# The delta rule stage of a two-block model: decayed query-key products on VectorE, decayed keys on ScalarE

## The chip, the cores and the metric

The kernel runs on one core of a Trainium2 chip. A core has TensorE (matmuls), VectorE, ScalarE and GpSimd, each with an instruction queue of its own, and SyncE, which issues the transfers here. The metric is the device time of one execution in microseconds (us), shown as the median of repeated runs. Beside the runs one execution was taken down by the hardware profiler; all rows below come from it.

## What is computed

The reference runs a sequence of 512 tokens with 1024 features through two blocks of layers in float32. The change lies in the gated delta rule of the second block, with 16 value heads, 8 query-key heads of 128 features and a chunk length of 64 in the reference. Cut to the rule, it reads:

```python
def gated_delta_rule(q, k, v, g, beta):
    """S_t = exp(g_t) (I - beta_t k_t k_t^T) S_{t-1} + beta_t k_t v_t^T,  o_t = S_t^T q_t."""
...
    g = jnp.cumsum(g, axis=-1)
    decay = jnp.exp(jnp.where(lower, g[..., :, None] - g[..., None, :], -jnp.inf))
    L = jnp.where(strict, jnp.einsum('bhncd,bhnsd->bhncs', kb, k) * decay, 0.0)
    T = lax.linalg.triangular_solve(eye + L, eye, left_side=True, lower=True, unit_diagonal=True)
    u = T @ vb
    w = T @ (kb * jnp.exp(g)[..., None])
    attn = jnp.einsum('bhncd,bhnsd->bhncs', q, k) * decay
    q_dec = q * jnp.exp(g)[..., None]
    k_dec = k * jnp.exp(g[..., -1:] - g)[..., None]
    def step(state, inp):
        v_new = u_n - jnp.einsum('bhcd,bhde->bhce', w_n, state)
        o = q_n @ state + a_n @ v_new
        state = state * gl_n + jnp.einsum('bhcd,bhce->bhde', k_n, v_new)
```

Here `attn` is the decayed query-key product, `q_dec` the decayed queries and `k_dec` the decayed keys. The kernel names them At, qd and kdec, and the decayed key product L is its Am. It uses chunks of 128.

## The kernel before

Activations are kept feature-major, as tiles of 128 features by 512 tokens. Each float32 matmul is made of three products of rounded halves (L145 to L147: high by high, low by high, high by low). A weight tile arrives by DMA, ScalarE casts it to its high half wh (L139) and VectorE subtracts to get the low half wl (L140). Below, a projection row is one such matmul of 128x512 of L145 to L147, and 24 of them make one output tile of a 1024-feature projection in a bank of PSUM.

The delta rule stage is `gdn`, from about 1875 to 2420 us of the span. It goes in eight groups `gi`, each of one query-key head and the two value heads that share it. The functions called for a group are:

- `stage_a`: the projections of q and k, the convolution (L1020 on ScalarE, three L1022 on VectorE, then the tanh L1015 on ScalarE and L1016 on VectorE, which make silu), the norms of q and k, the masked key-key and query-key products (L1100 on TensorE, L1101 on VectorE, into tiles gt), the decay e on ScalarE (L1117, L1119, into a tmp), then for each of two heads Am (L1121, L1122 on VectorE) and At (L1123), the exponentials for qd (L1124), qd (L1127 on GpSimd, one product per head), and the inversion of the unit triangular matrix. The last begins with 15 pairs of small VectorE steps (L1144 product, L1146 sum), has DMAs to shuffle blocks (L1133 to L1156), and ends with small matmuls on TensorE (L1169 to L1207).
- `stage_v`: the projections, the convolution and the silu of the two value heads into cv, transposed on TensorE (L1221) and copied by ScalarE (L1222).
- `stage_b`: the recurrence over four chunks of 128 tokens. A chunk makes kdec (L1240, not for the last chunk), then on TensorE L1248 (state times keys), R on VectorE (L1251), L1254, vnew on ScalarE (L1257), L1261 (kdec times vnew, the new state's sum), L1264 and L1265 (outputs from qd and At), the new state on VectorE (L1271, L1274) and the output oT on ScalarE (L1276). kdec has one buffer, so that the kdec of a chunk waits until L1261 of the chunk before has read the old one.
- `stage_z`, `stage_g` and `stage_o`: the gate, the output norm and the output projection. `norms` transposes (L1036) on TensorE, sums squares on ScalarE (L1038), makes the inverse root on VectorE (L1041 to L1051), and brings it back either by broadcast matmuls (L1057; the first two groups of `stage_a` and the last group's outputs) or by a transpose L1062, a copy L1064 and two DMAs. `stage_g` multiplies the outputs by the gate (L1287, L1288). In `stage_o` the output projection of a group fills a bank, and L1305 on VectorE adds it into h and frees the bank.

Program order is `stage_a(0)`, `stage_a(1)`, `stage_v(0)`, and then for each group `stage_v(gi+1)`, `stage_a(gi+2)`, `stage_b(gi)`, `stage_z(gi)`, `stage_g(gi)`, `stage_o(gi-1)`. A scheduler lays out each engine's queue when the program is built, from this order and its own priorities, and some steps carry a raised priority (`high_priority`: the norms' chain, R, St and L1305). Each engine then runs its queue strictly in order. PSUM banks come from four pools: three for projections ("acc"), two of "sa", two of "sb", one of "mg". The `tmp` tiles rotate through four buffers.

Of the kernel before, what the change touches and what calls it, by code (L numbers as in the profile page):

```python
# [12 lines left out]
AF = mybir.ActivationFunctionType  # L13
# [6 lines left out]
D, S, DFF, KT, P = 1024, 512, 2816, 8, 128  # L20
# [420 lines left out]
def c4(ap, c):  # L441
    return ap[:, c * P:(c + 1) * P]
# [524 lines left out]
def gdn(self, feed0, gate, tail):  # L967
    nc, tc, A = self.nc, self.tc, self.A
    with tc.tile_pool(name="gd", bufs=1) as gd, tc.tile_pool(name="gdd", bufs=1, space=bass.MemoryType.DRAM) as dr:
        def T(name, shape=(P, S), dtype=F32, bufs=None):  # L970
            return gd.tile(list(shape), dtype, name=name, bufs=bufs)
# [103 lines left out]
        def stage_a(gi):  # L1075
# [14 lines left out]
            knat = T("knat", (P, 4, P), bufs=2)  # L1090
# [5 lines left out]
            kkm, qkm = T("gt", bufs=2), T("gt", bufs=2)  # L1096
# [12 lines left out]
            ekd = T("ekd", (P, 2, 4), bufs=2)  # L1109
# [3 lines left out]
            Am, At = T("Am", (P, 8, P), bufs=2), T("At", (P, 8, P), bufs=2)  # L1113
            for a in range(2):
                e = self.tmp()
                for c in range(4):
                    nc.scalar.activation(c4(e, c), gbc[:, a, c * P:(c + 1) * P], AF.Relu, scale=-1.0,  # L1117
                                         bias=gcol[:, c, hs[a]:hs[a] + 1])
                nc.scalar.activation(e, e, AF.Exp, scale=-1.0)  # L1119
                m = Am[:, a * 4:(a + 1) * 4, :]  # L1120
                nc.vector.tensor_mul(m.rearrange("p c i -> p (c i)"), kkm, e)  # L1121
                nc.vector.tensor_mul(m, m, bcol[:, :, hs[a]:hs[a] + 1].to_broadcast([P, 4, P]))  # L1122
                nc.gpsimd.tensor_mul(At[:, a * 4:(a + 1) * 4, :].rearrange("p c i -> p (c i)"), qkm, e)  # L1123
            nc.scalar.activation(gbc, gbc, AF.Exp, bias=ln_qs)  # L1124
            qd = T("qd", (P, 2, S), bufs=2)
            for a in range(2):
# [106 lines left out]
        def stage_b(gi, d, vn):  # L1233
            hs, U, k = d["hs"], d["U"], d["k"]
            oT = T("oT", (P, 2, S))
            St = None
            for c in range(4):
                if c < 3:
                    kdec = T("kdec", (P, 2, P))
                    nc.gpsimd.tensor_mul(kdec, d["knat"][:, c:c + 1, :].to_broadcast([P, 2, P]),  # L1240
                                         d["ekd"][:, :, c:c + 1].to_broadcast([P, 2, P]))
                pp = self.bank("sb")
                if c == 0:
                    R = vn[:, 0]
                else:
                    R = T("R", (P, 2, P))
                    for a in range(2):
                        nc.tensor.matmul(c4(pp, a), c4(k, c), St[:, a, :], start=True, stop=True)  # L1248
                    with tc.high_priority():
                        for a in range(2):  # L1250
                            nc.vector.scalar_tensor_tensor(R[:, a, :], c4(pp, a), neg[:, c, hs[a]:hs[a] + 1],  # L1251
                                                           vn[:, c, a, :], op0=ALU.mult, op1=ALU.add)
                for a in range(2):
                    nc.tensor.matmul(c4(pp, 2 + a), U[:, a * 4 + c, :], R[:, a, :], start=True, stop=True)  # L1254
                w = T("vnew", (P, 2, P), bufs=2)
                for a in range(2):
                    nc.scalar.activation(w[:, a, :], c4(pp, 2 + a), AF.Copy, scale=bcol[:, c, hs[a]:hs[a] + 1])  # L1257
                po = self.bank("sb")
                if c < 3:
                    for a in range(2):  # L1260
                        nc.tensor.matmul(c4(po, 2 + a), kdec[:, a, :], w[:, a, :], start=True, stop=True)  # L1261
                for a in range(2):
                    if c:
                        nc.tensor.matmul(c4(po, a), St[:, a, :], d["qd"][:, a, c * P:(c + 1) * P], start=True, stop=False)  # L1264
                    nc.tensor.matmul(c4(po, a), w[:, a, :], d["At"][:, a * 4 + c, :], start=c == 0, stop=True)  # L1265
                if c < 3:
                    sn = T("St", (P, 2, P), bufs=2)
                    with tc.high_priority():
                        for a in range(2):
                            if c:  # L1270
                                nc.vector.scalar_tensor_tensor(sn[:, a, :], St[:, a, :], d["egl"][:, a, c:c + 1],  # L1271
                                                               c4(po, 2 + a), op0=ALU.mult, op1=ALU.add)
                            else:
                                nc.vector.tensor_copy(sn[:, a, :], c4(po, 2 + a))  # L1274
                    St = sn
                nc.scalar.copy(oT[:, :, c * P:(c + 1) * P], po[:, 0:256].rearrange("p (a d) -> p a d", a=2))  # L1276
            return oT
# [29 lines left out]

        og, last = {}, []
        st = {gi: stage_a(gi) for gi in range(2)}
        vs = {0: stage_v(0)}  # L1310
        for gi in range(8):
            if gi < 7:
                vs[gi + 1] = stage_v(gi + 1)
            if gi < 6:
                st[gi + 2] = stage_a(gi + 2)
            if gi == 0:
                self.late()
            oT = stage_b(gi, st.pop(gi), vs.pop(gi))
            z = stage_z(gi)
            og[gi] = stage_g(gi, oT, z)  # L1320
            if gi:
                stage_o(gi - 1, og.pop(gi - 1))
# [436 lines left out]
```

## Time and profile before

| | us |
|---|---|
| runs, median of 3 | 2773.18 |
| runs, lowest and highest | 2771.43, 2778.86 |
| profiled execution | 2774.42 |
| its span in the trace | 2772.6 |
| mean granted TensorE clock over the span | 0.987 |

The span is the time from the first to the last instruction in the trace; the profiled execution's own time holds 1.8 us more around it. Busy times are given by engine: PE is TensorE, PEld its weight loads, DVE VectorE, ACT ScalarE, POOL GpSimd. An engine's idle time is put down to the event that ended it, its releaser, written with an arrow. PEclk, the granted clock, is given as a share of full speed, 1.00 being the level of 2.4 GHz and 0.50 that of 1.2.

### The profile page before, as it was taken

To read this page: it belongs to the slowest core of one execution; us is meant where nothing else is said; L and a number is where in the kernel's file an instruction comes from. 1 tells how busy PE (TensorE), PEld (TensorE's weight loads), DVE (VectorE), ACT (ScalarE), POOL (GpSimd) and SP (SyncE) were. 2 spreads that over 40 slices of the span, in tenths; PEclk is the share of its full clock that TensorE was granted. 3 is DMA by queue.
4 is the path that set the end of the run, shared out by engine and by line. 5 is a ranking of instruction groups with operands and counts; after the bars stand their busy time and mean duration, and the time that the engine had idled before them with its cause. 6 is when DMAs were issued, how large, how long until landed. Compare 5 with 4: busy or idle time off the path is not lost. (4 is left out here: it accounts for less than half of the span.)

```text
span 2772.6 us, 38299 instructions
## 1 busy us (share of the span) xinstructions
PE 2684.4 (97%) x14903; PEld 2194.3 (79%) x14903; DVE 1723.4 (62%) x3065; ACT 1197.1 (43%) x2200; POOL 237.5 (9%) x224
## 2 busy tenths in 40 slices
PE   8999999999999999999899999998999999999998
PEld 6888878788888888887778888877778788787776
DVE  6454577764545744447965444468777777777776
ACT  4222244532323422224364222255655555577774
POOL 0000002000000000003410000022111111110001
PEclk9999999999999999999999999999999999999999
DMA  5343432243443433223212333223333333132221
GB/s 183 116 144 107 127 97 77 76 144 115 137 119 110 133 112 102 91 91 92 68 39 90 96 94 99 88 75 100 93 107 100 100 114 102 48 101 69 77 66 63
DMA packets 106709, 274.60 MB, mean 99 GB/s; under 512 B 35464, under 2 KB 39552, under 8 KB 106528
## 3 DMA queue, kind: packets, MB, share of 16 engines
q1 hardware_dynamic: 106528, 272.15, 32.5%
q8 instruction: 118, 1.93, 0.3%
q14 instruction: 63, 0.52, 0.1%
HBM read 267.79 MB, written 4.31 MB: 98 GB/s over the span
## 5 line engine op out<-in xcount | busy, mean ns | idle before, releaser
L145 PE MATMUL acc<-xh,wh 128*128 128x512 f32 (+2 forms) x2320 | 913.0, 394 | 18.4 <-ACT xh L186 8.1
L146 PE MATMUL acc<-xl,wh 128*128 128x512 f32 (+1 forms) x2320 | 903.6, 390 | 3.3 <-POOL xl L151 2.4
L147 PE MATMUL acc<-xh,wl 128*128 128x512 f32 (+1 forms) x2320 | 902.4, 389 | 1.7 <-DVE wl L140 1.7
L139 ACT CAST wh<-raw 128x1024 fp32r<-128x1024 f32 (+3 forms) x430 | 438.9, 1022 | 1076.2 <-PE acc L146 714.6
L140 DVE TENSOR_TENSOR wl<-raw,wh 128x1024 fp32r<-128x1024 f32 (+2 forms) x410 | 488.8, 1193 | 71.3 <-ACT wh L139 70.7
L145 PEld LDWEIGHTS acc<-xh,wh 128*128 128x128 f32 (+1 forms) x2320 | 437.8, 189 | 108.4 <-ACT xh L186 8.1
L146 PEld LDWEIGHTS acc<-xl,wh 128*128 128x128 f32 x2320 | 437.7, 189 | 92.7 <-issue 3.7
L147 PEld LDWEIGHTS acc<-xh,wl 128*128 128x128 f32 x2320 | 436.9, 188 | 91.2 <-DVE wl L140 3.2
L146 PE MATMUL acc<-al,wh 128*128 128x512 f32 (+1 forms) x720 | 278.2, 386 | 0.0
L147 PE MATMUL acc<-ah,wl 128*128 128x512 f32 (+1 forms) x720 | 277.7, 386 | 0.0
L145 PE MATMUL acc<-ah,wh 128*128 128x512 f32 (+1 forms) x720 | 277.4, 386 | 0.0
L249 DVE SCALAR_TENSOR_TENSOR h<-acc,h 128x512 f32<-128x512 f32 x128 | 88.4, 690 | 215.3 <-PE acc L147 214.9
L289 DVE TENSOR_TENSOR tmp<-acc,rstd 128x512 f32<-128x512 f32 x88 | 60.8, 691 | 239.2 <-PE acc L147 239.2
L287 DVE TENSOR_TENSOR tmp<-acc,rstd 128x512 f32<-128x512 f32 x88 | 60.8, 691 | 176.3 <-PE acc L147 176.2
L146 PEld LDWEIGHTS acc<-al,wh 128*128 128x128 f32 x720 | 135.2, 188 | 28.8 <-DVE al L151 0.8
L145 PEld LDWEIGHTS acc<-ah,wh 128*128 128x128 f32 x720 | 135.2, 188 | 28.1
L147 PEld LDWEIGHTS acc<-ah,wl 128*128 128x128 f32 x720 | 135.2, 188 | 28.0
L140 POOL TENSOR_TENSOR wl<-raw,wh 128x1024 fp32r<-128x1024 f32 (+1 forms) x20 | 47.8, 2393 | 872.2 <-ACT wh L139 861.4
L145 PE MATMUL acc<-ogh,wh 128*128 128x512 f32 (+1 forms) x256 | 104.4, 409 | 5.4 <-DVE h L1305 3.0
L147 PE MATMUL acc<-ogh,wl 128*128 128x512 f32 (+1 forms) x256 | 99.1, 388 | 0.0
L146 PE MATMUL acc<-ogl,wh 128*128 128x512 f32 (+1 forms) x256 | 99.1, 388 | 0.0
L150 ACT CAST ah<-tmp 128x512 fp32r<-128x512 f32 x88 | 54.9, 624 | 63.8 <-DVE tmp L290 63.8
(450 smaller groups left out, 3462.9 us busy)
## 6 DMA issues: line engine op xcount, KB each, us to landing
raw<-in_wi_dram SPq DMA_DIRECT2D x176, 512.0 KB, 3.6
raw<-in_wo_dram SPq DMA_DIRECT2D x64, 512.0 KB, 3.5
raw<-in_ada_w_dram SPq DMA_DIRECT2D x48, 512.0 KB, 3.6
raw<-in_a_in_dram SPq DMA_DIRECT2D x48, 512.0 KB, 4.1
raw<-in_b_in_dram SPq DMA_DIRECT2D x24, 512.0 KB, 3.6
raw<-in_wo_dram SPq DMA_DIRECT2D x24, 384.0 KB, 3.1
raw<-in_a_out_dram SPq DMA_DIRECT2D x16, 512.0 KB, 3.7
big<-rd SPq DMA_DIRECT2D x13, 512.0 KB, 5.6
```

What stands on the lines that cost most here:

```text
L139: nc.scalar.copy(wh[:, :n], raw[:, :n])
L140: self.lo_eng.tensor_tensor(wl[:, :n], raw[:, :n], f32(wh[:, :n]), op=ALU.subtract)
L145: nc.tensor.matmul(out, ah, bh, start=start, stop=False)
L146: nc.tensor.matmul(out, ah, bl, start=False, stop=False)
L147: nc.tensor.matmul(out, al, bh, start=False, stop=stop)
L150: self.nc.scalar.copy(hi, x)
L249: nc.vector.scalar_tensor_tensor(self.h[m], ps, scale(m), self.h[m], op0=ALU.mult, op1=ALU.add)
L287: nc.vector.tensor_mul(t, pg, rstd)
L289: nc.vector.tensor_mul(u, pu, rstd)
```

## The change

At (L1123) moves from GpSimd to VectorE, with the same operands and shape. kdec, one GpSimd product of 128x256 for both heads (L1240), becomes two ScalarE copies of 128x128, each with a scale per partition taken from ekd (L1241). GpSimd keeps qd, and no other line changes. A group has two At, and three chunks with a kdec: 16 products and 24 kdec (48 copies) in the stage.

```diff
--- before.py
+++ after.py
@@ -1120,7 +1120,7 @@
                 m = Am[:, a * 4:(a + 1) * 4, :]
                 nc.vector.tensor_mul(m.rearrange("p c i -> p (c i)"), kkm, e)
                 nc.vector.tensor_mul(m, m, bcol[:, :, hs[a]:hs[a] + 1].to_broadcast([P, 4, P]))
-                nc.gpsimd.tensor_mul(At[:, a * 4:(a + 1) * 4, :].rearrange("p c i -> p (c i)"), qkm, e)
+                nc.vector.tensor_mul(At[:, a * 4:(a + 1) * 4, :].rearrange("p c i -> p (c i)"), qkm, e)
             nc.scalar.activation(gbc, gbc, AF.Exp, bias=ln_qs)
             qd = T("qd", (P, 2, S), bufs=2)
             for a in range(2):
@@ -1237,8 +1237,8 @@
             for c in range(4):
                 if c < 3:
                     kdec = T("kdec", (P, 2, P))
-                    nc.gpsimd.tensor_mul(kdec, d["knat"][:, c:c + 1, :].to_broadcast([P, 2, P]),
-                                         d["ekd"][:, :, c:c + 1].to_broadcast([P, 2, P]))
+                    for a in range(2):
+                        nc.scalar.activation(kdec[:, a], d["knat"][:, c], AF.Copy, scale=d["ekd"][:, a, c:c + 1])
                 pp = self.bank("sb")
                 if c == 0:
                     R = vn[:, 0]
```

Since each queue is laid out anew, other instructions move too. Three places follow. The first is VectorE's queue in the ramp, while the second group's Am and At are made beside the first group's inversion (L1144, L1146) and ahead of the first value heads' silu (L1016). Before, At is not in it:

```order
L1146 TENSOR_REDUCE ui<-mt 128x2x2
L1122 TENSOR_TENSOR Am<-Am,gbcol 128x512
L1144 TENSOR_TENSOR mt<-ui,big 128x2x3x10
L1016 SCALAR_TENSOR_TENSOR cv<-tmp,cv 128x512
L1146 TENSOR_REDUCE ui<-mt 128x2x3
L1121 TENSOR_TENSOR Am<-gt,tmp 128x512
L1144 TENSOR_TENSOR mt<-ui,big 128x2x3x11
L1122 TENSOR_TENSOR Am<-Am,gbcol 128x512
L1146 TENSOR_REDUCE ui<-mt 128x2x3
L1144 TENSOR_TENSOR mt<-ui,big 128x2x3x12
L1146 TENSOR_REDUCE ui<-mt 128x2x3
L1016 SCALAR_TENSOR_TENSOR cv<-tmp,cv 128x512
```

With the change:

```order
L1144 TENSOR_TENSOR mt<-ui,big 128x2x3x10
L1122 TENSOR_TENSOR Am<-Am,gbcol 128x512
L1146 TENSOR_REDUCE ui<-mt 128x2x3
L1123 TENSOR_TENSOR At<-gt,tmp 128x512
L1144 TENSOR_TENSOR mt<-ui,big 128x2x3x11
L1121 TENSOR_TENSOR Am<-gt,tmp 128x512
L1146 TENSOR_REDUCE ui<-mt 128x2x3
L1122 TENSOR_TENSOR Am<-Am,gbcol 128x512
L1144 TENSOR_TENSOR mt<-ui,big 128x2x3x12
L1123 TENSOR_TENSOR At<-gt,tmp 128x512
L1146 TENSOR_REDUCE ui<-mt 128x2x3
L1016 SCALAR_TENSOR_TENSOR cv<-tmp,cv 128x512
```

Both At now stand in VectorE's queue; two L1121, two L1122, two L1123 and six chain steps come ahead of the first L1016 of cv, where there had been one Am alone. The second L1016 follows after one more chain step, and two L1022 of x come next, ahead of the three of cv; before, the first of cv came two rows after the second L1016.

The second place is TensorE's queue at the output norms of the first group: L1062 transposes the inverse roots (nr), and the last L1036 of the same outputs oT stands some rows ahead of it. Before:

```order
L145 MATMUL acc<-xh_97,wh 128x512
L146 MATMUL acc<-xl_105,wh 128x512
L1062 MATMUL sb<-ident,nr_15115 8x128
L1221 MATMUL sb<-ident,cv 128x128 x4
L147 MATMUL acc<-xh_97,wl 128x512
L1221 MATMUL sb<-ident,cv 128x128 x4
```

With the change:

```order
L145 MATMUL acc<-xh_104,wh 128x512
L1062 MATMUL sb<-ident,nr_15118 8x128
L1221 MATMUL sb<-ident,cv 128x128 x8
L146 MATMUL acc<-xl_112,wh 128x512
L147 MATMUL acc<-xh_104,wl 128x512
L1036 MATMUL sa<-ident,x_15294 128x128 x4
```

Between the last L1036 of oT and this L1062 there are 21 projection rows before and 45 with the change. At the same norms of the next group the count goes from 62 to 22, and there L1169 to L1189 of an inversion and the products L1100 now stand among the rows.

The third place is VectorE's queue around the first four L1305, which add the first group's output projection into h. Before:

```order
L1121 TENSOR_TENSOR Am<-gt,tmp 128x512
L1287 TENSOR_TENSOR oT<-oT,zg 128x512
L1122 TENSOR_TENSOR Am<-Am,gbcol 128x512
L1121 TENSOR_TENSOR Am<-gt,tmp 128x512
L1305 SCALAR_TENSOR_TENSOR h_89<-acc,mod_273,h_89 128x512
L1122 TENSOR_TENSOR Am<-Am,gbcol 128x512
L1305 SCALAR_TENSOR_TENSOR h_90<-acc,mod_273,h_90 128x512
L1016 SCALAR_TENSOR_TENSOR zg<-zg,acc 128x512
L1041 TENSOR_SCALAR nr_15788<-nr_15788 128x8
L1305 SCALAR_TENSOR_TENSOR h_91<-acc,mod_273,h_91 128x512
```

With the change:

```order
L1305 SCALAR_TENSOR_TENSOR h_89<-acc,mod_273,h_89 128x512
L1041 TENSOR_SCALAR nr_15794<-nr_15794 128x8
L1161 STREAM_TRANSPOSE tcp<-uc 128x256
L1305 SCALAR_TENSOR_TENSOR h_90<-acc,mod_273,h_90 128x512
L1043 TENSOR_SCALAR nr_15795<-nr_15794 128x8
L1287 TENSOR_TENSOR oT<-oT,zg 128x512
L1044 TENSOR_SCALAR nr_15795<-nr_15795 128x8
L1094 TENSOR_TENSOR x_15294<-x_15294,big 128x512
L1305 SCALAR_TENSOR_TENSOR h_91<-acc,mod_273,h_91 128x512
```

Before, two L1121 and one L1122 stand ahead of the first L1305; with the change three L1305 follow in nine rows, and the fourth comes 14 rows later, right ahead of the first L1121.

## Rows read from the trace of the kernel before

**Rows 1.** The page, part 1: busy time, share of the span, instructions of each engine.

```profile
PE 2684.4 (97%) x14903; PEld 2194.3 (79%) x14903; DVE 1723.4 (62%) x3065; ACT 1197.1 (43%) x2200; POOL 237.5 (9%) x224
```

**Rows 2.** Windows: stretch, us, busy PE, PEld, DVE, ACT, POOL, PEclk, DMA share, GB/s.

```profile
1875.00:1965.00 90.00, 76.18 (x494) 62.20 (x493) 78.56 (x167) 48.73 (x121) 12.87 (x10) 0.91 0.37 105
1940.00:1950.00 10.00, 6.81 (x24) 5.35 (x25) 8.80 (x22) 5.75 (x10) 0.00 (x0) 0.62 0.21 45
2000.00:2020.00 20.00, 17.02 (x83) 13.98 (x82) 19.00 (x57) 10.09 (x35) 6.00 (x4) 0.91 0.25 80
2050.00:2060.00 10.00, 7.58 (x26) 5.94 (x27) 8.79 (x15) 2.25 (x5) 2.82 (x2) 0.83 0.08 13
2060.00:2400.00 340.00, 336.29 (x2804) 271.65 (x2802) 257.23 (x599) 177.66 (x468) 41.61 (x41) 1.00 0.35 102
```

**Rows 3.** Groups of instructions, 1880 to 2420: busy us, mean ns, idle before.

```profile
L1122 DVE TENSOR_TENSOR Am<-Am,gbcol 128x512 f32<-128x512 f32 x16 | 19.1, 1199 | 0.2
L1121 DVE TENSOR_TENSOR Am<-gt,tmp 128x512 f32<-128x512 f32 x16 | 16.3, 1025 | 0.3 <-ACT tmp L1119 0.3
L1127 POOL TENSOR_TENSOR qd<-x,big 128x512 f32<-128x512 f32 x16 | 25.2, 1592 | 1.2 <-ACT cv L1020 1.2
L1123 POOL TENSOR_TENSOR At<-gt,tmp 128x512 f32<-128x512 f32 x16 | 24.4, 1532 | 65.8 <-ACT tmp L1119 50.0 <-DVE gt L1101 15.8
```

**Rows 4.** Line L1122: ns least/median/most, first and last start.

```profile
L1122 DVE TENSOR_TENSOR Am<-Am,gbcol x16: 677/1108/1786, 1910.9 to 2315.5; 128x512 f32<-128x512 f32 x16
```

**Rows 5.** Timeline of the ramp: start us, us, instruction [idle before <- releaser].

```profile
1933.89 1.72 DVE L1122 TENSOR_TENSOR Am<-Am,gbcol 128x512 f32<-128x512 f32 x1
1936.77 1.75 DVE L1016 SCALAR_TENSOR_TENSOR cv<-tmp,cv 128x512 f32<-128x512 f32 x1
...
1933.80 1.26 POOL L1123 TENSOR_TENSOR At<-gt,tmp 128x512 f32<-128x512 f32 x1 [0.63 <-ACT tmp L1119]
1935.02 2.95 POOL L1127 TENSOR_TENSOR qd<-x,big 128x512 f32<-128x512 f32 x2
...
1932.98 0.39 PE L146 MATMUL acc<-xl,wh 128*128 128x512 f32 x1
1933.21 0.39 PE L147 MATMUL acc<-xh,wl 128*128 128x512 f32 x1
1938.58 1.11 PE L1221 MATMUL sb<-ident,cv 128*128 128x128 f32 x4 [4.98 <-DVE cv L1016]
1941.62 1.11 PE L1221 MATMUL sb<-ident,cv 128*128 128x128 f32 x4 [1.93 <-DVE cv L1016]
1944.30 0.77 PE L145 MATMUL acc<-xh,wh 128*128 128x512 f32 x1 [1.56 <-DVE cv L1022]
```

**Rows 6.** Line L1144, a step of the inversion chain.

```profile
L1144 DVE TENSOR_TENSOR mt<-ui,big x120: 155/226/1312, 1926.1 to 2347.4; 128x4 f32<-128x4 f32 x8, 128x6 f32<-128x6 f32 x8, 128x8 f32<-128x8 f32 x8, 128x10 f32<-128x10 f32 x8
```

**Rows 7.** Waits of TensorE, 1880 to 2420: us in total, times, longest.

```profile
PE sa L1057 <- DVE nr L1051: 1.8, 1, 1.8
```

**Rows 8.** Timeline of TensorE at the first group's output norms.

```profile
2009.24 0.37 PE L1062 MATMUL sb<-ident,nr 128*8 128x128 f32 x1 [2.98 <-DVE ui L1146]
```

**Rows 9.** Timeline of VectorE and TensorE at the first output projection.

```profile
2048.24 1.79 DVE L1122 TENSOR_TENSOR Am<-Am,gbcol 128x512 f32<-128x512 f32 x1
...
2052.41 0.50 PE L145 MATMUL acc<-ogh,wh 128*128 128x512 f32 x1 [2.98 <-DVE h L1305]
```

**Rows 10.** Line L1257, vnew on ScalarE.

```profile
L1257 ACT ACTIVATE vnew<-sb,gbcol x64: 343/362/398, 1976.9 to 2393.2; 128x128 f32<-128x128 f32 x64
```

**Rows 11.** Timeline of one chunk: vnew and the products that read kdec.

```profile
1990.84 0.62 ACT L1257 ACTIVATE vnew<-sb,gbcol 128x128 f32<-128x128 f32 x2
...
1991.91 0.71 PE L1261 MATMUL sb<-vnew,kdec 128*128 128x128 f32 x4
```

**Rows 12.** Waits of ScalarE, 1880 to 2420.

```profile
ACT wh L139 <- PE acc L146: 73.5, 41, 10.1
```

**Rows 13.** Timeline of VectorE in the last group.

```profile
2399.83 0.93 DVE L1288 SCALAR_TENSOR_TENSOR oT<-sb,pk,oT 128x256 f32<-128x256 f32 x2
```

## The prediction

> **What bounds the kernel.** I read the page's first part, then the windows, then TensorE's waits, then timelines of three places. TensorE is busy for 97% of the span [rows 1]. The change touches only the delta rule stage, about 1875 to 2420 us. There the windows show two regimes [rows 2]: from 2060 to 2400 TensorE is busy 336.3 of 340 us at full clock, so at most 3.7 us can come back; before 2060 it idles at a few places and the granted clock falls behind them (0.62 in 1940 to 1950, between the levels of 1.2 and 2.4 GHz). In the ramp, 1875 to 1965, VectorE is busy 78.56 of 90 us and TensorE 76.18: the ramp waits for VectorE.
>
> Why VectorE is late shows where GpSimd runs. A two-input product on 512 columns takes VectorE 0.68 us when nothing meets it (the minimum of L1122) [rows 4]. The two Am lines average 1025 and 1199 ns over 16 each [rows 3], so they lose 16 x (1.025 + 1.199 - 2 x 0.68) = 13.8 us. The timeline shows to whom: L1122 begins at 1933.89 and takes 1.72 us while GpSimd runs At from 1933.80 for 1.26; L1016, begun at 1936.77 beside qd, takes 1.75 [rows 5]. Such a meeting costs VectorE 1.72 - 0.68, about 1.05 us. Short steps are hit too: L1144 has a median of 226 ns and a maximum of 1312 [rows 6].
>
> **The change part by part.** All is added to the profiled execution's own 2774.42 us (span 2772.6 and 1.8 around it), which lies 1.24 us over the median of the three runs, 2773.18.
>
> *At to VectorE.* GpSimd loses 16 products of 1.53 us [rows 3], 24.4 us for which no wait of TensorE stands. VectorE gains 16 x 0.68 = 10.9 us. Against that go the meetings with At: at 1.05 us each, and none to two per product, 0 to 34 us; the 13.8 us above are shared with qd (also 16 products), which makes about 7 the likelier size. So VectorE's total moves by a few us; what counts is where. From 2060 on VectorE is busy 257 of 340 us [rows 2] and TensorE sets the pace, so I cost the products there at nothing; if that cover went, 2 x 0.68 us a group would show, about 8 us over six groups.
>
> Place 1, the ramp. TensorE waits 4.98, 1.93 and 1.56 us for VectorE at two sets of transposes L1221 and at a bank [rows 5]. In the new order the first L1016 of cv stands behind one more L1121, its L1122, both At and two more steps of the chain L1144/L1146: 4 x 0.68 + 2 x 0.45 = 3.6 us more (0.45: an L1144 at its median and as much for L1146). Two meetings with At on the way (one with a chain step, and the L1122 at 1933.89) save 2.1. The qd meetings stay. So the first L1016 ends 1.5 us later, near 1940.0; the second follows with one chain step between and ends near 1940.9, about 0.6 earlier than the 1941.6 at which its transposes start now. But then two L1022 of x and three chain steps go ahead of cv's L1022, some 2.0 us by the prices above, so the bank that TensorE waits for at 1944.30 comes free 1.4 us later. The 1.8 us wait for L1051 [rows 7] goes, since nine more projection rows stand ahead of L1057; those rows are then missing ahead of L1221, so it is a wait moved, not won. **Term: +1.4**, bounds -2 (qd misses the late products) and +4.
>
> Place 2, near 2009. L1062, the transpose of the first group's output norms, waits 2.98 us [rows 8]; VectorE is busy 19.0 of the 20 us around it, with four GpSimd products in them [rows 2]. In the new order 45 projection rows, not 21, stand between the oT transposes and L1062. Rows follow each other at 0.23 us (1932.98, 1933.21) [rows 5]: 24 x 0.23 = 5.5 us of cover, more than the 2.98. L1051 itself moves back by some 2 us (an L140 and L1022 steps stand ahead of it), which still fits. The clock in these 20 us is 0.91 [rows 2]: 20 x 0.09 = 1.8 us. **Term: -2.98 - 1.8 = -4.8**, bounds -4.8 and +2.
>
> Place 3, near 2052. The first L1305, which frees a bank for the output projection, stands behind Am work that GpSimd meets (L1122: 1.79 us at 2048.24), and TensorE waits 2.98 us [rows 9]; the clock of 0.83 in the 10 us around it [rows 2] is another 1.7. In the new order four L1305 come ahead of the first Am. What is late next: the second group's L1062, whose cover falls from 62 projection rows to 22, or 5.1 us, with the inversion's L1169 to L1189 now among them. VectorE has about as much to do there as TensorE has rows and small products, so I give 1.5 us back. **Term: -4.7 + 1.5 = -3.2**, bounds -4.7 and +2.
>
> *kdec to ScalarE.* 48 activations of 128x128; the nearest row, vnew, has 362 ns [rows 10], so 17.4 us of ScalarE, which in 2060 to 2400 is busy 178 of 340 us [rows 2]. Each kdec past a group's first must wait until TensorE has read the one before (there is one buffer). GpSimd did that waiting with only kdec and qd behind; on ScalarE the casts L139, the evictions and oT stand behind. From one vnew's start to the end of its L1261 it is about 1.8 us (1990.84 to 1991.91 + 0.71 [rows 11]), of which vnew has 0.6, so a wait of 1.2 us, 16 times: 19 us of queue time. The casts have slack: they wait 73.5 us for TensorE to release weight buffers [rows 12]. **Term: 0**, bounds 0 and +19. The operand kdec is ready in time: its first half needs only knat and ekd, its second a wait that ends a chunk before its use.
>
> *qd alone on GpSimd.* Its queue no longer stops at kdec, so qd starts with its own inputs. No wait of TensorE stands for it: 0.
>
> *The end.* In the last group L1057 now has 8 rows of output products before the next step, not 24. Behind it come the L1288 pair (0.93 us [rows 13]), a cast and a subtraction; by estimate 2.9 us in all, with two L1305 among them, against 7 x 0.23 = 1.6 us of rows: **+1.3**, bounds 0 and +3.
>
> The sum is +1.4 - 4.8 - 3.2 + 0 + 1.3 = -5.3: 2769.1 on the profiled execution's scale, 2767.9 on the median's. I say 2768.
>
> A rule speaks against the change. In the ramp VectorE is busy 78.56 of 90 us and ScalarE 48.73 [rows 2]. The Trainium skill, Perfetto Trace Analysis, section Optimizing Scalar/DVE Operations, advises to hand work from a saturated VectorE to ScalarE or even GpSimd; At goes the other way here. By that rule alone the products ahead of place 1 would count in full, 3.6 instead of 1.5 us, and places 2 and 3 would keep their waits, a sum near +5. The trace speaks against that reading: the meetings in rows 5 and 9 cost more than the products that replace them.
>
> **Rivals.** *The ramp speeds up too* (more than forecast). If VectorE's work is the ramp's whole limit, its four At products cost 2.7 us, and their meetings, at the mean loss of 13.8 / 16 = 0.86 a product, give back 3.5; and the clock of 0.62, 3.8 us over 10 us, comes partly back. Then place 1 is about -4 instead of +1.4: 2762. For it: VectorE's 87%. Against: the new order puts both At ahead of cv's L1016.
>
> *Waits reappear elsewhere* (no gain). The order changes on every engine for 500 us; waits of 2 to 3 us with 1.7 us of clock behind them hang on where one norm or one L1305 stands. If places 2 and 3 lose their gain to two such new ones, the sum is +2.7: 2776. For it: the cover of 22 rows at place 3. Against: 45 rows at place 2, and L1305 moved up.
>
> *ScalarE's queue holds TensorE* (slower). The kdec that waits for L1261 holds the casts and evictions behind it. If each of the 16 waits of 1.2 us reached TensorE, +19 us and a sum of +14: 2787; it decides the sign beyond the bound below from about 0.9 us each. For it: evictions on ScalarE free TensorE's banks, of which the projections have three. Against: the slack of rows 12, and ScalarE's half idle time.
>
> *The change is hidden.* If the steady groups, 98.9% busy, were all, nothing would show: 2773 to 2774. It shares its class with the second rival.
>
> **How the numbers follow.** The forecast has 0.48, its own range 2763 to 2773. The faster ramp has 0.2, waits elsewhere (with the hidden case) 0.2, ScalarE's queue 0.12. A measurement of this kernel tells about 0.3%, 8.3 us, from no change: under 2764.9 or over 2781.5. Faster: nearly all of the 0.2 and a fifth of the forecast, 0.30. Slower: the 0.12 alone, since 2776 is inside. Same: 0.58. The range runs from 2758 (the bounds of places 1 to 3 good together, but for a clock that comes back half) to 2781 (waits elsewhere, with the end and place 1 near their bounds); it leaves out the slower rival and the tails, some 0.2.
>
> **What would show it.** In the new profile L1121 and L1122 average under 0.9 us, L1123 stands on VectorE at about 0.7, and L1144 keeps a few values over 1.2 (qd). TensorE's wait for L1051 near 1919 is gone, the one at L1221 grows to about 8 us, and no wait over 1 us stands at L1062 near 2010 or at the first L1305 near 2050; the clock in those windows is 1.00. ScalarE waits 15 to 20 us for L1261 at L1241, with no TensorE wait for L1241, L139 or L1020. I am wrong if TensorE's idle time before 2060 is not 3 to 8 us less, or if the time from 2060 to the end of the stage has grown by more than 3 us.

## The result and the profile after

The changed kernel takes 2761.80 us, the median of four runs (2759.31 to 2763.99), where the kernel before took 2774.89 beside it: a ratio of 0.995, 95% interval 0.9937 to 0.9963. That is 13.1 us less. It lies inside the whole range, though under the forecast's own 2763 to 2773; the fall is more than twice the 5.3 us of the sum, and "faster by over 0.3%", which happened, had been given only 0.30. The profiled execution took 2762.07 us with a span of 2760.3.

Busy time by engine over the span, part 1 of the page after, against [rows 1]:

```profile
PE 2674.5 (97%) x14903; PEld 2186.6 (79%) x14903; DVE 1719.7 (62%) x3081; ACT 1211.2 (44%) x2248; POOL 197.4 (7%) x184
```

VectorE has 16 instructions more and 4 us less. The windows after, columns as in [rows 2], with two more stretches:

```profile
1875.00:1965.00 90.00, 75.47 (x529) 61.68 (x528) 79.55 (x182) 51.91 (x129) 7.79 (x7) 0.92 0.37 104
1880.00:1900.00 20.00, 17.44 (x85) 13.95 (x84) 18.98 (x39) 17.56 (x44) 0.00 (x0) 1.00 0.35 107
1930.00:1950.00 20.00, 9.30 (x32) 7.14 (x31) 18.83 (x38) 9.27 (x17) 3.51 (x2) 0.66 0.18 46
2000.00:2020.00 20.00, 18.40 (x97) 15.00 (x96) 19.69 (x59) 10.03 (x35) 1.28 (x1) 1.00 0.27 84
2050.00:2060.00 10.00, 10.00 (x48) 8.19 (x47) 7.36 (x8) 4.09 (x6) 3.02 (x3) 1.00 0.32 79
2060.00:2400.00 340.00, 335.63 (x2823) 273.18 (x2823) 260.10 (x616) 189.37 (x515) 20.05 (x18) 1.00 0.36 100
```

The ramp still waits (9.30 of 20 us busy from 1930 to 1950), the clock near 2010 and 2055 is full, and from 2060 to 2400 TensorE's busy share is as it was. The groups of instructions after, 1880 to 2420, against [rows 3]:

```profile
L1127 POOL TENSOR_TENSOR qd<-x,big 128x512 f32<-128x512 f32 x16 | 24.9, 1574 | 77.0 <-DVE At L1123 27.8 <-ACT kdec L1241 25.8 <-DVE Am L1121 18.4
L1241 ACT ACTIVATE kdec<-knat,ekd 128x128 f32<-128x128 f32 x48 | 17.0, 401 | 7.8 <-PE sb L1261 7.3 <-DVE knat L1091 0.4
L1123 DVE TENSOR_TENSOR At<-gt,tmp 128x512 f32<-128x512 f32 x16 | 16.3, 1022 | 2.2 <-PE sb L1265 2.2
L1122 DVE TENSOR_TENSOR Am<-Am,gbcol 128x512 f32<-128x512 f32 x16 | 14.6, 914 | 0.0
L1121 DVE TENSOR_TENSOR Am<-gt,tmp 128x512 f32<-128x512 f32 x16 | 11.0, 685 | 3.1 <-ACT tmp L1119 3.0
```

L1121 is free of GpSimd (1025 to 685 ns); L1122 and At itself still meet qd. The timeline of the ramp and of the first group's output norms after, against [rows 5] and [rows 8]:

```profile
1932.81 3.51 POOL L1127 TENSOR_TENSOR qd<-x,big 128x512 f32<-128x512 f32 x2 [27.76 <-DVE At L1123]
...
1933.58 1.63 DVE L1122 TENSOR_TENSOR Am<-Am,gbcol 128x512 f32<-128x512 f32 x1
1935.13 1.33 DVE L1144 TENSOR_TENSOR mt<-ui,big 128x72 f32<-128x72 f32 x1
1937.12 0.68 DVE L1016 SCALAR_TENSOR_TENSOR cv<-tmp,cv 128x512 f32<-128x512 f32 x1
...
1937.85 1.97 PE L1221 MATMUL sb<-ident,cv 128*128 128x128 f32 x8 [7.45 <-DVE cv L1016]
1943.07 0.77 PE L145 MATMUL acc<-xh,wh 128*128 128x512 f32 x1 [3.25 <-DVE cv L1022]
2011.52 0.27 PE L1062 MATMUL sb<-ident,nr 128*8 128x128 f32 x1 [1.60 <-DVE ui L1146]
```

TensorE waits 7.45 and 3.25 us in the ramp and 1.60 at L1062, and not at all at the first L1305. Three waits are new: 0.77 to 0.79 us at the L1062 of three later groups (2186.0, 2251.3 and 2316.5).

### The profile page after: what moved, and what is told of

Same layout as the page of the kernel before. It is cut to its first block, busy times and chain, and to the rows that moved or that the text cites. A ratio compares the mean times of both kernels' runs of the same rounds, so it can differ in the third digit from the quotient of the medians.

```text
span 2760.3 us, 38266 instructions
## 1 busy us (share of the span) xinstructions
PE 2674.5 (97%) x14903; PEld 2186.6 (79%) x14903; DVE 1719.7 (62%) x3081; ACT 1211.2 (44%) x2248; POOL 197.4 (7%) x184
## 3 DMA queue, kind: packets, MB, share of 16 engines
q8 instruction: 118, 1.93, 0.3%
## 5 line engine op out<-in xcount | busy, mean ns | idle before, releaser
L139 ACT CAST wh<-raw 128x1024 fp32r<-128x1024 f32 (+3 forms) x430 | 439.3, 1022 | 1070.0 <-PE acc L146 706.8
L140 DVE TENSOR_TENSOR wl<-raw,wh 128x1024 fp32r<-128x1024 f32 (+2 forms) x410 | 489.9, 1196 | 80.9 <-ACT wh L139 76.9
L140 POOL TENSOR_TENSOR wl<-raw,wh 128x1024 fp32r<-128x1024 f32 (+1 forms) x20 | 47.8, 2392 | 872.3 <-ACT wh L139 861.2
```

Source lines behind the costliest of these rows:

```text
L139: nc.scalar.copy(wh[:, :n], raw[:, :n])
L140: self.lo_eng.tensor_tensor(wl[:, :n], raw[:, :n], f32(wh[:, :n]), op=ALU.subtract)
```

## The experiments

All runs, with the kernel before timed beside each set (medians 2776.35, 2777.02 and 2777.25). The ratio is to the kernel before; differences between runs of different sets are taken from the ratios.

| run | edit | median us | ratio [95%] |
|---|---|---|---|
| c_before | none | 2774.51 | 0.9994 [0.9984, 1.0004] |
| c_after | the change again | 2762.88 | 0.9948 [0.9936, 0.9959] |
| e1_at_only | At moved, kdec not | 2768.57 | 0.9968 [0.9956, 0.9979] |
| e2_kdec_only | kdec moved, At not | 2776.00 | 1.0001 [0.9991, 1.0011] |
| e6_ghost_at | change, At on GpSimd as well | 2772.56 | 0.9986 [0.9978, 0.9995] |
| e8_at_blank | before, At zeros | 2768.82 | 0.9968 [0.9955, 0.9980] |
| e5_two_kdec | change, two kdec buffers | 2764.74 | 0.9956 [0.9943, 0.9970] |
| e7_kdec_twice | change, kdec written twice | 2763.05 | 0.9954 [0.9942, 0.9967] |
| e4_v_first | change, values first | 2760.61 | 0.9946 [0.9933, 0.9958] |
| e3_qd_too | change, qd on VectorE too | 2756.53 | 0.9932 [0.9918, 0.9945] |
| e11_kdec_alone | the same, kdec on GpSimd | 2761.70 | 0.9947 [0.9934, 0.9959] |
| e10_qd_v_first | qd on VectorE, values first | 2751.38 | 0.9908 [0.9895, 0.9922] |

**Both kernels again.** No edit.

> The kernel before once more, for a second profile. The waits of 1.81, 4.98, 1.93, 1.56, 2.98 and 2.98 us before 2060 should be there to 0.1 us, since the same queues meet the same inputs. The clock is open: if it falls by chance, the loss of 3.4 us between 1880 and 1900 (0.83) may be absent or another; if it belongs to this kernel, it is 0.83 again. The span should lie in 2769 to 2780 us.

> The changed kernel once more. It should repeat 2759 to 2764 us, with 10 to 15 us less than the kernel before. What is open is the clock between 1880 and 1900: in the profile of before it was 0.81 and 0.85 (3.4 us lost), in that of the change 1.00, though the same instructions stand there with the same waits. If it falls by chance, this profile or the next one of before shows the other value, and some 3 us of the 12.4 us between the two profiles are no effect of the change. If it belongs to the change, it is 1.00 here again and below 0.9 whenever before is profiled.

The change repeats: 13.5 us less. The clock between 1880 and 1900 is no effect of it. The window of before, then of the change's second profile:

```profile
1880.00:1900.00 20.00, 17.76 (x75) 14.04 (x75) 17.65 (x36) 16.52 (x42) 0.00 (x0) 0.83 0.33 107
```

```profile
1880.00:1900.00 20.00, 17.76 (x77) 14.16 (x76) 18.30 (x36) 15.10 (x42) 0.00 (x0) 0.83 0.33 107
```

It is 0.83 for the change here where it was 1.00 above, and 0.91 in the second profile of before. The waits repeat (in before's second profile 1.81, 4.98, 1.93, 1.56, 2.99, 2.98). From the first L1002 to the last row of L1057 the stage lasted 528.2 and 529.0 us in the two profiles of before, 517.3 and 519.7 in those of the change: 8.5 to 11.7 us of the 13 are in the stage, and up to 3.4 of that is this chance (the 8.5 are between the two profiles with 0.83). TensorE's waits from 1880 to 2400, added, are 23.0 us in both profiles of before and 19.4 and 20.0 in those of the change. The clock lost (1.00 less the granted clock, added over windows of 10 us) is 11.9 us in both of before, 6.9 and 10.2 in those of the change. What is left lies outside the stage, where both kernels' queues are the same, and goes with the clock: behind the last L1057 the profiles of before take 359.3 and 359.2 us with 9.8 lost in each, those of the change 356.9 and 358.6 with 6.7 and 8.4.

**One part alone.** In e1 L1240 is as before, in e2 L1123:

```diff
# e1_at_only, against before
-                nc.gpsimd.tensor_mul(At[...], qkm, e)
+                nc.vector.tensor_mul(At[...], qkm, e)
# e2_kdec_only, against before
-                    nc.gpsimd.tensor_mul(kdec, knat.to_broadcast(...), ekd.to_broadcast(...))
+                    for a in range(2):
+                        nc.scalar.activation(kdec[:, a], knat, AF.Copy, scale=ekd[:, a])
```

> At on VectorE, kdec still one GpSimd product. Theory (the order that At's move brings takes the waits at L1062 and L1305 away): the queue of TensorE is nearly that of the change (37 and 18 projection rows ahead of the first two output L1062, where the change has 45 and 22), so nearly all of the gain is here: 2761 to 2767 us. Rival (GpSimd's queue, in which qd stood behind the waiting kdec, was the limit): less than half of the gain, 2768 us or more.

> kdec on ScalarE, At still on GpSimd. Theory: kdec is worth nothing either way. TensorE's order is that of before (21 and 62 rows ahead of L1062), the 2.98 us waits at the first output L1062 and at the first L1305 are there again: 2771 to 2778 us. Rival one (ScalarE's queue is held by the waits for L1261, hidden in the change by its gain): 2780 us or more. Rival two (kdec was the gain): 2767 us or less.

At's move alone is worth 7.8 us, just short of what theory asked (2768.57 against 2767 at most). Its time lies in the rival's range of 2768 or more, but it is more than half of the gain, which the rival denied. kdec alone is worth nothing, and the waits stand as before: TensorE's timeline of e2, at the first output L1062, the first L1305 and an L1189:

```profile
2006.71 0.27 PE L1062 MATMUL sb<-ident,nr 128*8 128x128 f32 x1 [3.50 <-DVE ui L1146]
2050.11 0.50 PE L145 MATMUL acc<-ogh,wh 128*128 128x512 f32 x1 [3.04 <-DVE h L1305]
2172.87 0.58 PE L1189 MATMUL mg<-tcp,Am 32*32 32x32 f32 x14 [3.63 <-issue]
```

Yet beside At's move kdec's is worth 5.7 us by the medians (e1 against c_after; no run of one lies among those of the other, and the stage in e1's profile, 525.0 us, is 5.3 to 7.7 longer). In e1 an L1288 takes 1.10 us beside a kdec on GpSimd (its least is 0.74), with St behind it in VectorE's queue and TensorE behind St:

```profile
2014.80 0.62 POOL L1240 TENSOR_TENSOR kdec<-knat,ekd 128x256 f32<-128x256 f32 x1 [16.22 <-PE sb L1261]
2014.87 1.10 DVE L1288 SCALAR_TENSOR_TENSOR oT<-big,pk,oT 128x512 f32<-128x512 f32 x1 [0.39 <-DMA big<-rd]
...
2017.02 0.71 PE L1248 MATMUL sb<-St,x 128*128 128x128 f32 x4 [0.75 <-DVE St L1274]
```

**Order against meetings.** e6 brings the meetings with At back into the change's order; e8 takes them out of the old order (16 GpSimd fills in the trace, 12 of them after 1880, and outputs without the part of each chunk's own keys).

```diff
# e6_ghost_at, against the change (lines after L1123 move by two)
                 nc.vector.tensor_mul(At[...], qkm, e)
+                gh = T("gh")
+                nc.gpsimd.tensor_mul(gh, qkm, e)
# e8_at_blank, against before
-                nc.gpsimd.tensor_mul(At[...], qkm, e)
+                nc.gpsimd.memset(At[...], 0.0)
```

> The change, with each At also computed by GpSimd from the same operands into a tile that nobody reads, so that VectorE has its new work and GpSimd meets it as before; TensorE's order is row for row that of the change at all output norms (45, 22, 24, 61, 61, 61, 12 rows). Theory (order decides): the meetings, up to 16 at about 1 us, cost VectorE some 14 us, of which only those ahead of the first L1016 of cv and at the first L1062 reach TensorE: 2 to 6 us over the change, 2764 to 2768 us, still faster than before. Rival (freedom from the meetings is the gain): all of it goes, 2773 us or more.

> The kernel before with GpSimd only filling At with zeros in place of the product, so that outputs lack the part of each chunk's own keys; the queues of TensorE and VectorE are row for row those of before, VectorE has no new work, and the meetings of VectorE with At are gone. It prices those meetings in the old order. If order decides, most of the waits stay: 4.98 falls by two meetings to about 2.9, the 2.98 at L1062 by two to about 0.9, the 2.98 at the first L1305 by one to about 2; in all 5 to 7 us less than before, 2769 to 2772 us, and less than the change gains. Rival (the meetings are all of the gain, and the change's order brings nothing): 2764 us or less, since here VectorE is spared the 10.9 us of products too.

e6 comes out 9.7 us over the change, still 3.8 under before and nearly where the rival put it. TensorE's timeline of e6 (L1223 is the L1221 of the others):

```profile
1941.18 1.97 PE L1223 MATMUL sb<-ident,cv 128*128 128x128 f32 x8 [9.31 <-DVE cv L1016]
...
2016.74 0.27 PE L1062 MATMUL sb<-ident,nr 128*8 128x128 f32 x1 [1.60 <-DVE ui L1148]
```

At L1062 it is the 1.60 us of the change, and there is no wait at the first output projection: there the order decides, as theory said. In the ramp and the steady groups the meetings cost: TensorE's waits from 1880 to 2400 are 26.0 us against 19.4 and 20.0 in the change and 23.0 before, and At takes VectorE 1492 ns in place of 1022:

```profile
L1123 DVE TENSOR_TENSOR At<-gt,tmp 128x512 f32<-128x512 f32 x16 | 23.8, 1492 | 2.2 <-PE sb L1267 2.2
```

So theory held at the two waits that it spoke of, and its "2 to 6 us" fell. e8 gains 8.2 us, more than the 5 to 7 expected and less than the rival's. Its timeline of TensorE:

```profile
1933.35 0.66 PE L1221 MATMUL sb<-ident,cv 128*128 128x128 f32 x4 [0.79 <-DVE cv L1016]
1938.32 1.11 PE L1221 MATMUL sb<-ident,cv 128*128 128x128 f32 x4 [4.31 <-DVE cv L1016]
...
2005.64 0.27 PE L1062 MATMUL sb<-ident,nr 128*8 128x128 f32 x1 [1.44 <-DVE ui L1146]
```

Of the 2.98 us at L1062 half is left, and the wait at the first L1305 is gone, here without any change of order. Either cause alone is enough at place 3. Taken together, the meetings brought back take 9.7 of the change's 13.5 us away, and At's taken out of the old order give 8.2: freedom from meetings is most of the gain.

**ScalarE's price.** A second buffer, and each kdec written twice:

```diff
# e5_two_kdec, against the change
-                    kdec = T("kdec", (P, 2, P))
+                    kdec = T("kdec", (P, 2, P), bufs=2)
# e7_kdec_twice, against the change: the two lines of L1240 and L1241 stand twice
```

> The change with a second buffer for kdec. ScalarE's wait at L1241 for L1261 (7.3 us in the change's profile) goes. Theory (that wait is covered): within 3 us of the change, 2759 to 2765 us. Rival (the waiting kdec holds oT and the casts, and TensorE with them): 2757 us or less.

> The change with each kdec written twice by ScalarE: 48 more copies of about 0.36 us, 17 us. It prices ScalarE's time in the stage. Theory (ScalarE has slack, the term 0): up to 4 us over the change, 2760 to 2767 us. Rival (ScalarE's queue reaches TensorE): 2770 us or more.

Against the change's 0.9948 both cost about 2 us or nothing (0.9956, 0.9954): 17 us more of ScalarE do not reach TensorE. Groups of e7, 1880 to 2420:

```profile
L1241 ACT ACTIVATE kdec<-knat,ekd 128x128 f32<-128x128 f32 x48 | 17.1, 402 | 6.6 <-PE sb L1263 6.5
L1243 ACT ACTIVATE kdec<-knat,ekd 128x128 f32<-128x128 f32 x48 | 17.0, 396 | 0.0
```

The second buffer did not take ScalarE's wait for L1261 away (6.9 us in e5), so that run is no test of that wait.

**No product left on GpSimd, and the ramp's order.** e3 moves qd, e11 then puts kdec back; e4 and e10 change the program order.

```diff
# e3_qd_too, against the change (e11_kdec_alone: this, and L1240 as before)
-                nc.gpsimd.tensor_mul(qd[:, a], q, gbc[:, a])
+                nc.vector.tensor_mul(qd[:, a], q, gbc[:, a])
# e4_v_first, against the change (e10_qd_v_first: against e3)
-        st = {gi: stage_a(gi) for gi in range(2)}
-        vs = {0: stage_v(0)}
+        st = {0: stage_a(0)}
+        vs = {0: stage_v(0)}
+        st[1] = stage_a(1)
```

> The change with qd on VectorE as well, so that GpSimd has no product in the stage. VectorE gains 16 x 0.68 = 10.9 us and loses its last meetings (L1122 1.63 and L1144 1.33 in the ramp, 2 us there). Theory (a meeting costs about what the product costs): within 3 us of the change, 2759 to 2766 us. Rival (the meetings cost more than the products everywhere, as the change's gain might say): 2757 us or less. Other rival (VectorE's load decides in the ramp): 2767 us or more.

> At and qd on VectorE, kdec back on GpSimd, where it is the only product. It tells why kdec's move was worth 5.7 us beside At's and nothing alone. Theory A (kdec's own meetings: 24 products of 0.62 us that hold VectorE's R, St and norms): 4 to 8 us over the run with no product on GpSimd, 2760 to 2765 us. Theory B (GpSimd's queue: qd stood behind the kdec that waits for L1261, and met VectorE at worse places): that goes here, so within 2 us of it, 2754 to 2759 us.

> The change with the first value heads' projection and silu placed in program order ahead of the second group's query-key work, so that cv's L1016 no longer stands behind the second group's Am and At. Theory (place 1 is a matter of queue order): the waits of 7.45 and 3.25 us at L1221 and at the bank and most of the clock loss behind them (0.66 over 20 us, 6.8 us) go, and some of it comes back at the first L1062, which has only 9 rows ahead of it: 2752 to 2759 us. Rival (the ramp is bound by VectorE's sum of work, whatever its order): the wait turns up at another place, 2760 to 2766 us.

> No products on GpSimd (qd on VectorE too) and the first value heads put ahead of the second group's query-key work. Theory: the ramp's waits go as in the run with the values first, where 7.45 and 3.25 became 1.55, and without meetings the waits that came back there (2.27, three of 1.00) shrink: 2748 to 2755 us, the fastest. Rival (the order at the output norms eats it): 2756 us or more.

e3 is 4 us faster than the change by the ratios (6 by the medians), though VectorE has 10.7 us more to do; the median falls just into the rival's range, while the two intervals still overlap. Groups of e3:

```profile
L1121 DVE TENSOR_TENSOR Am<-gt,tmp 128x512 f32<-128x512 f32 x16 | 11.0, 686 | 4.9 <-ACT tmp L1119 4.9
L1123 DVE TENSOR_TENSOR At<-gt,tmp 128x512 f32<-128x512 f32 x16 | 11.0, 685 | 0.0
L1122 DVE TENSOR_TENSOR Am<-Am,gbcol 128x512 f32<-128x512 f32 x16 | 10.9, 683 | 0.0
L1127 DVE TENSOR_TENSOR qd<-x,big 128x512 f32<-128x512 f32 x16 | 10.7, 685 | 0.0
```

Every product takes its least time now, and TensorE's waits from 1880 to 2400 fall from 19.4 us to 13.9 (without the last L1057, which lies behind 2400 in the others). e11 loses 4 to 5 us of it by the medians, as theory A said, but its interval overlaps that of e3, and its trace does not show theory A's way: TensorE waits 15.0 us, and kdec's meetings cost VectorE 2.6. Of the 5.2 us that the stage takes longer (516.8 against 511.6), 3.6 are clock (10.4 lost against 6.8). So what kdec costs with no other product on GpSimd is not shown. e4 clears the ramp (its wait at L1221 is 1.55 us and the clock from 1930 to 1950 is 1.00), but gains only 0.6: the waits come back later, as its rival said. TensorE's timeline of e4:

```profile
1935.36 0.66 PE L1221 MATMUL sb<-ident,cv 128*128 128x128 f32 x4 [1.55 <-DVE cv L1016]
...
2050.54 0.27 PE L1062 MATMUL sb<-ident,nr 128*8 128x128 f32 x1 [2.27 <-DVE nr L1051]
...
2171.16 0.50 PE L145 MATMUL acc<-ogh,wh 128*128 128x512 f32 x1 [1.00 <-DVE h L1305]
```

Without products on GpSimd the same move is worth 5 to 7 us: e10 takes 2751.38 us, 25.9 less than before, and beats both kernels. Its window of the ramp, against 9.30 of 20 in the change:

```profile
1930.00:1950.00 20.00, 18.53 (x87) 14.36 (x86) 19.19 (x48) 8.07 (x26) 0.00 (x0) 1.00 0.27 70
```

## Why the prediction was right in direction and short in size

*The scale.* The forecast stood on a median of 2773.18 us; over 24 runs it is 2776.35. On that scale the same sum would have said 2771, so the forecast time came closer than the sum did, by the luck of a low median. What has to be explained is the fall: 5.3 us forecast, 13.1 and 13.5 measured.

*At to VectorE.* I added what each VectorE instruction from 1880 to 2400 took above the least of its line and shape, where that was over 0.3 us. Every such instruction overlaps one on GpSimd in the trace, and its loss is put to that one (in us):

| run | in all | beside At or its copy | beside qd | beside kdec |
|---|---|---|---|---|
| before | 23.1 | 15.0 | 6.3 | 1.8 |
| e8, At zeros | 6.7 | 0 | 5.3 | 1.4 |
| e1, At moved | 14.6 | - | 13.3 | 1.3 |
| the change | 13.0 | - | 12.5 | - |
| e6, At on both | 26.0 | 13.9 | 12.1 | - |
| e11, kdec alone | 3.4 | - | - | 2.6 |
| e3, none | 1.4 | - | - | - |

What is left in the change, e11 and e3 stands beside L337, a GpSimd step of the norm behind the stage. So At's meetings cost 15.0 us, twice the 7 of the step "which makes about 7 the likelier size", but qd's meetings, which the prediction let stay, doubled when At was gone. At's move alone saves 8.5 of the 23.1: the size of 7 came nearly true because two misses cancel. The forecast that VectorE's total would move by a few us holds. L1122 and At average 914 and 1022 ns, not under 900 and about 700, because qd meets them. A step that failed is the one that cost the steady groups at nothing: in each of three of them e6 falls 0.8 to 0.9 us further behind the change.

*Place 1, +1.4.* The waits were 10.28 us in all [rows 5, 7] and are 10.70: +0.4, and the clock is 0.66 where it was 0.74 and, in the second profile, 0.66. The wait for L1051 went and the one at L1221 grew, to 7.45 us where about 8 was said. One working was off: the first L1016 met no qd this time, and ended 10.6 us after the chain's first L1144 (12.4 before), but the two L1022 of x ahead of cv's gave that back at the bank.

*Place 2, -4.8.* The wait fell from 2.98 to 1.60 only, since L1051 was put back further than 2 us, behind two L140 and six L1022: from L1041 to its end it is 7.7 us where it was 3.6. The clock's 1.8 came back. Measured: -3.2.

*Place 3, -3.2.* All of -4.7 came, and the 1.5 us that I gave back at the next L1062 did not: no wait stands there. But the 1.7 of clock in it is no sure gain: in the second profile of before the same wait of 2.98 us leaves the clock at 1.00 from 2040 to 2060. *The end, +1.3:* the last L1057 waits 1.33 us in both kernels, so 0. Together these places make -7.5, or -5.8 without that 1.7, where e1 has 7.8. TensorE's waits from 1880 to 2060 fell from 19.8 to 15.2 us, which is inside the 3 to 8 that the prediction asked for.

*kdec to ScalarE, 0.* This is the term that was mis-sized: beside At's move it is worth 5.7 us by the medians. Its bounds, 0 and +19, left out a gain, because kdec was looked at as GpSimd's waiting and ScalarE's load, and not as one more product of GpSimd that meets VectorE. The cost side held: ScalarE waits 7.3 us for L1261, not 15 to 20, and e7 shows its slack. How the gain comes about is only partly settled. The meetings are a small part: kdec costs VectorE 1.3 us in e1 and 2.6 in e11. TensorE's waits from 1880 to 2400 are 22.0 us in e1 and 19.4 and 20.0 in the change, with the 0.75 shown above and 1.40 with no releaser among those of e1, and the clock lost is 10.2 us in e1, 6.9 and 10.2 in the change. Three pairs differ in kdec alone: before and e2, e1 and the change, e11 and e3. In each of them the stage, less TensorE's waits and less the clock lost outside of these, is by estimate 1.6 to 2.8 us shorter with kdec on ScalarE; no row shows where. Why kdec alone is worth nothing in the old order was not settled either, but e2's profile has 2.4 us more of waits than before (at L1189 3.63 us in place of 1.89 to 2.00) and 3.4 us more of lost clock, which may hide its gain.

*The rivals.* The time is that of "the ramp speeds up too", but not by its mechanism: the ramp did not speed up. "Waits reappear elsewhere" happened in small, with the three new waits at L1062, 2.4 us in all, and "ScalarE's queue" did not happen. The rule that speaks against the change (the Trainium skill, Perfetto Trace Analysis, Optimizing Scalar/DVE Operations) would have made it slower, and does not decide here; the section itself says only that such a move may make sense. The same section's caution that GpSimd and VectorE share a read port, so that offloading between them might not help, decides: e3 moves 16 more products back to a VectorE that is busy 79.55 of the ramp's 90 us in the change, and is no slower.

## What to carry to other kernels

Where a GpSimd product runs beside VectorE's two-input work, price it at what VectorE loses, not at what GpSimd is busy: compare the mean of a line with its least time, and look which GpSimd product each slow instruction overlaps. Expect a product that stays on GpSimd to meet more once the others are gone, as qd did. Taking such products back to VectorE cost nothing here, and a better program order paid only once the meetings were gone. When a scheduler lays out the queues anew, check each long wait of TensorE by its own row after the change, since order and meetings can each remove it.

## What was not expected of the hardware

The waits repeat to a few hundredths of a microsecond between executions, but the clock that follows them does not: behind the same waits of 1.1 us near 1884, the granted clock of 1880 to 1900 was 0.83, 0.91, 0.83 and 1.00 in four profiles of the two kernels. One profile of each is thus good for the waits, and not for 3 us of time. The Trainium skill, TensorE: Matmul & The Clock Gate, What's actually happening, says that the gate's window runs freely and that the same kernel varies with it from run to run; the four values agree.

GpSimd's fills of At held nobody in e8. Two of them stand beside two L1287, products with two inputs in SBUF, which took 0.68 us each; in before the second of the same two, begun while At's product ran, took 1.72. Before, then e8:

```profile
2001.37 0.68 DVE L1287 TENSOR_TENSOR oT<-oT,zg 128x512 f32<-128x512 f32 x1
2001.38 3.52 POOL L1123 TENSOR_TENSOR At<-gt,tmp 128x512 f32<-128x512 f32 x2
2002.03 1.72 DVE L1287 TENSOR_TENSOR oT<-oT,zg 128x512 f32<-128x512 f32 x1
```

```profile
1999.30 0.99 POOL L1123 MEMSET At<- 128x512 f32 x2
1999.31 0.68 DVE L1287 TENSOR_TENSOR oT<-oT,zg 128x512 f32<-128x512 f32 x1
1999.97 0.68 DVE L1287 TENSOR_TENSOR oT<-oT,zg 128x512 f32<-128x512 f32 x1
```

The Trainium skill, SBUF — State Buffer, Who interferes with whom, says that a VectorE instruction with two SBUF inputs contends with a GpSimd instruction that reads SBUF, not with one that only writes it; the trace agrees.

TensorE stopped for 2.00 us in the middle of L1189 at 2174 in before, with no releaser in the profile, and for 3.63 in e2; the change has 0.53 in one profile, 1.03 and 0.57 in the other at such places. The DMA records tell what it probably waits for. From 1880 to 2420 all profiles together have 15 such stops of over 0.45 us, the 1.40 of e1 among them, and each ends 1.27 to 1.60 us after a 16 KB transfer of the queue named "instruction" has landed (in before at 2172.93, with TensorE going on at 2174.41), though a profile has only 34 or 35 such transfers there. So these look like waits for TensorE's next instructions. What makes them longer in one run than in another stays open.
